# Two transformer layers on one Trainium2 core: the norm at each channel mixer's entrance taken apart, and its low parts moved behind each scaled tile

## The chip, the cores and the metric

One core of one Trainium2 chip runs the whole program. The metric is the time of one execution on the device in microseconds; the times given are medians of runs, and the profile is of one execution of its own.

## What is computed

A trunk of two layers on a sequence of 1024 tokens with 1024 features. Each layer is a token mixer (forgetting attention in layer 0, gated linear attention in layer 1) and a dense channel mixer, each behind an RMS norm that is scaled and shifted by a vector. The change lies where the channel mixer begins:

```python
def rms_norm(x, g):
    xf = x.astype(jnp.float32)
    y = xf * lax.rsqrt(jnp.mean(xf * xf, axis=-1, keepdims=True) + EPS)
    return (y * g.astype(jnp.float32)).astype(x.dtype)

def modulate(h, shift, scale):
    return h * (1.0 + scale[:, None, :]) + shift[:, None, :]

def swiglu(h, w_in, w_out):
    gate, up = jnp.split(h @ w_in, 2, axis=-1)
    return (jax.nn.silu(gate) * up) @ w_out
```

## The kernel before

Features lie on the 128 partitions, in eight blocks of 128; tokens lie along the free axis, in two halves of 512. An exact float32 product is made of three: each operand is kept as a high part that TensorE takes at full rate and a low part, the rest. `mm3` issues the three: L290 is weight high by tile high, L291 weight high by tile low, L292 weight low by tile high. One matmul is 128x128 weights by 128x512. So a tile's low part is first read by L291 and a weight's low part first by L292. Parts of activations are made by `split_t`: the high part on ScalarE (L1436, L1439), the low part on VectorE (L1437 without a shift, L1440 with one). Parts of weights come the same way, L174 on ScalarE and L175 on VectorE, from tiles that the feed loads.

The channel mixer (`ffn`, L1397) multiplies in a scheme of the Strassen kind: token halves and feature halves make four blocks, B11 and B21 of the first half of the tokens, B12 and B22 of the second, each of four tiles. Differences T1 = B12 − B11 and T2 = B22 − T1, and later T3 and T4, feed products that need fewer multiplications. The first group of hidden features is done without the scheme, in eight *plain tiles* (`plain_tile`, L1587), each of 24 matmuls into one bank of PSUM: three on the first half of the tokens, then four on the second, and one more on the first. The scheduler interleaves plain tiles where their operands come late. Their ends, L1605 and L1576, add or multiply from PSUM on VectorE.

The scaled tiles need the norm. Squares of the features are added up (`SumSq`, L741), for this norm into two roots; `sums` (L751) multiplies each root with a column of ones, four matmuls of one column each (L756), all into one tile sp. L699 on VectorE and a power on GpSimd (L700) make the four columns of inverse roots; L709 spreads them into rb, 128x512 in PSUM, with four matmuls. `normed` (L1432) is x by a column by rb, on VectorE.

For the first half of the tokens that has been done before the plain tiles begin. For the second half, `rms_rows` and `second_half` come ahead of the plain tiles in the code, and `GK=(4, 7)` holds products of the second plain tile behind the sums and rb: from its fourth step on they are issued behind the sums, from its seventh behind rb. `second_half` makes B12 and B22 (tile yb, then its parts), the differences from GpSimd (L1474) and VectorE (L1476), and the parts of T1 and T2. A scheduler puts the instructions of each engine into one fixed order, by data and by these gates. Each engine then runs its own list in that order.

PSUM has eight banks: six in the ring pj, two in psr; the plain tiles' ring pin uses them all.

Of the kernel before, what the change touches and what calls it, by code (L numbers as in the profile page):

```python
# [9 lines left out]
F32 = mybir.dt.float32  # L10
# [43 lines left out]
def trunk(ctx, tc, x, c, ada_w, ada_b, norm1_g, norm2_g, ffn_w_in, ffn_w_out,  # L54
          fox_w_in, fox_b_f, fox_w_out, gla_w_in, gla_w_a2, gla_b_a, gla_g_o,
          gla_w_out, final_g, out, dbg=None, stop=None):
    nc = tc.nc
# [51 lines left out]
    def psl(t, n=1):  # L109
        return slice(t * P, (t + n) * P)  # L110
# [51 lines left out]
    ones = cst.tile([P, 1], F32, name="ones")  # L162
# [126 lines left out]
    def mm3(ps, ah, al, bh, bl, start, stop):  # L289
        nc.tensor.matmul(ps, ah, bh, start=start, stop=False)  # L290
        nc.tensor.matmul(ps, ah, bl, start=False, stop=False)  # L291
        nc.tensor.matmul(ps, al, bh, start=False, stop=stop)  # L292
# [128 lines left out]
    def last_of(e):  # L421
        return next(i for i in reversed(nc.cur_bb.bb.instructions) if i.engine == ENG[e])
# [243 lines left out]
    def last_ins():  # L666
        return nc.cur_bb.bb.instructions[-1]
# [19 lines left out]

    sp_ins, rb_ins, root_ins = [], [], {}
    LATE1 = 7
    GK = (4, 7)  # L690
    SPM, RBM = (3, 4)

    def rms_cols(ss, nm, psr, n=4):

        ss.sums(psr)
        sp = ss.sp
        sp_ins.append(last_ins())
        rs = sm.tile([P, n], F32, tag="rs", name=f"rs{nm}")
        nc.vector.tensor_scalar(rs, sp, 1.0 / D, EPS, op0=ALU.mult, op1=ALU.add)  # L699
        nc.gpsimd.tensor_tensor(rs, rs, mhalf[:, 0:n], op=ALU.pow)  # L700
        root_ins.update(D=last_of("D"), G=last_of("G"))
        return rs

    def rms_rows(ss, nm, psr):

        rs = rms_cols(ss, nm, psr)
        rb = psr([P, HALF], F32, f"rb{nm}")
        for t in range(4):
            nc.tensor.matmul(rb[:, psl(t)], rs[:, t:t + 1].to_broadcast([P, P]), ident, start=True, stop=True)  # L709
        rb_ins.append(last_ins())  # L710
        return rb
# [29 lines left out]
    class SumSq:  # L741


        def __init__(self, v, hf, late, one=True):
            w = slice(256 * (hf % 2), 256 * (hf % 2) + 256) if hf > 1 else slice(0, HALF)
            self.v = [v[i][:, w] for i in ((1, 3, 2, 5, 7, 6, 3, 4) if hf else range(8))]
            self.late = late
            self.n = 2 if hf > 1 else 4
            self.roots = [self.v[0]] if one else [self.v[0], self.v[6]]

        def sums(self, psr):  # L751

            self.sp = psr([P, self.n], F32, "sp")
            for r in self.roots:
                for t in range(self.n):
                    nc.tensor.matmul(self.sp[:, t:t + 1], r[:, psl(t)], ones, start=r is self.roots[0] and t == 0,  # L756
                                     stop=r is self.roots[-1] and t == self.n - 1)

        def __call__(self, m, xk):
            v = self.v  # L760
# [29 lines left out]
    sr, tr, orr, pj = ps_rings(2, 3, 1, 2)  # L790
# [307 lines left out]
    for n, (d, hf) in enumerate(rest0):  # L1098
# [23 lines left out]
        if n in late_tr:  # L1122
            tp, i = late_tr[n]
# [273 lines left out]
    def ffn(l, oh, xs, slots, nm, mid, norm_end, each=None):  # L1397
# [32 lines left out]
        def normed(y, k, hf, rb):  # L1430

            nc.vector.scalar_tensor_tensor(y, xs[k][:, hsl(hf)], acol(l, 1, k), rb, op0=ALU.mult, op1=ALU.mult)  # L1432

        def split_t(t, y, shift=None):
            if shift is None:
                nc.scalar.copy(hi(t), y)  # L1436
                nc.vector.tensor_sub(lo(t), y, hi(t).bitcast(F32))  # L1437
# [15 lines left out]
        last_chunk(4, 4, oh, xs, l, 2, nm, sv, norm, one=False)  # L1453
        dump(f"xa{l}", xs)
        sg = opr_["sg"]
        rb = rms_rows(ss1[0], f"{l}11", psr)
        block("B22", H_SL[0:4])
        block("B12", H_SL[4:8])
        block("T1", H_SL[8:12])
        block("T2", H_SL[12:16])  # L1460
        B12, B22, T1, T2 = b["B12"], b["B22"], b["T1"], b["T2"]
        yv_ = Views(slots["to"], 2, [HALF], f"yb{l}").v
        y12, y22 = yv_[:4], yv_[4:]
        y11, y21 = ya[:4], ya[4:]

        def second_half():
            for k in range(4):
                normed(y12[k], k, 1, rb)
                split_t(B12[k], y12[k], sh(k))
            for k in range(4):  # L1470
                normed(y22[k], k + 4, 1, rb)
                split_t(B22[k], y22[k], sh(k + 4))
            for k in range(4):
                nc.gpsimd.tensor_sub(y11[k], y12[k], y11[k])  # L1474
                split_t(T1[k], y11[k])
                nc.vector.tensor_sub(y11[k], y22[k], y11[k])  # L1476
                split_t(T2[k], y11[k], sh(k + 4))
# [101 lines left out]
        B11, B21 = b["B11"], b["B21"]  # L1579


        pin = Ring(psp, list(pj.q) + list(psr.q))
        gs = [Group(*g) for g in GROUPS]
        second_half()
        wgs = [[[None, None], [None, None]] for _ in range(2)]

        def plain_tile(kind, m, hf, after=()):  # L1587
            wg = wgs[kind]
            ps = pin([P, HALF], F32, f"p{l}")
            for k in range(8):  # L1590
# [629 lines left out]
```

## Time and profile before

| | |
|---|---|
| runs | 2376.99, 2379.86, 2381.57 us; median 2379.86 |
| the profiled execution | 2379.58 us |
| its span | 2377.9 us |
| mean granted TensorE clock | 0.997 |
| instructions | 35,724 |

In the rows, PE is TensorE's matmuls, PEld its weight loads, DVE VectorE, ACT ScalarE, POOL GpSimd. A row of the timeline has start, duration, engine, line, operation, output and inputs, shape, and how many instructions are drawn together; in brackets stands the idle time ahead of it and what ended it. A row of the waits has the total, how often and the longest, in us. A window has each engine's busy time with the number of instructions, the granted clock (1.00 is full speed), and the DMA's share and rate. Times count from the start of the span; the stretch of the change lies near 655 us in layer 0 and near 1723 us in layer 1.

### The profile page before, as it was taken

How to read it: one execution, taken by the hardware profiler on the slowest of the kernel's cores; microseconds unless marked ns; L12 is line 12 of the kernel's file. 1: busy time of each engine (PE TensorE's matmuls, PEld its weight loads, DVE VectorE, ACT ScalarE, POOL GpSimd, SP SyncE). 2: the span in 40 equal slices, each digit the busy share in tenths (PEclk: the TensorE clock that was granted, in tenths of full speed). 3: DMA queues.
4: the chain of work that ended last, by engine and by line, in shares of the span. 5: the costliest groups of instructions: out<-in, count | busy, mean ns of one | idle time of the engine just before them, and what ended most of it. 6: DMA issues, size and time to landing. Idle time of an engine off the chain costs nothing.

```text
span 2377.9 us, 35724 instructions
## 1 busy us (share of the span) xinstructions
PE 2352.7 (99%) x12256; PEld 2004.9 (84%) x12256; DVE 1780.2 (75%) x2992; ACT 1129.3 (47%) x2178; POOL 1042.7 (44%) x976
## 2 busy tenths in 40 slices
PE   8999999999999999999999999999999999999998
PEld 7988888888888888888888889898888888888888
DVE  6577787886698878876788775655697877865787
ACT  6666566575443333345325655443444333345326
POOL 1334444533435666653363321212336666643262
PEclk9999999999999999999999999999999999999999
DMA  7423333332425544457665332334434544457664
GB/s 250 152 80 115 106 120 94 120 125 98 143 101 181 180 164 171 161 189 255 230 210 168 104 108 86 98 110 140 144 102 157 181 151 151 151 192 256 229 199 147
DMA packets 336366, 363.47 MB, mean 153 GB/s; under 512 B 24924, under 2 KB 278008, under 8 KB 336184
## 3 DMA queue, kind: packets, MB, share of 16 engines
q1 hardware_dynamic: 336184, 361.18, 45.6%
q8 instruction: 97, 1.59, 0.3%
q14 instruction: 85, 0.70, 0.1%
HBM read 268.22 MB, written 92.86 MB: 152 GB/s over the span
## 4 chain that ended last, share of the span: by engine, by line
PE 85%; DVE 8%; ACT 2%; issue 2%; DMA 2%; POOL 1%; SPq 1%; DVEq 0%; POOLq 0%; ACTq 0%
PE p_b L292 16%; PE p_b L290 16%; PE p_b L291 16%; PE o_b L1230 2%; PE t_b L1216 2%; PE qk_b L290 1%; PE qk_b L291 1%; PE qk_b L292 1%; PE vps_b L292 1%; PE vps_b L290 1%; PE vps_b L291 1%; PE gr_b L290 1%; PE s_b L1184 1%; PE gr_b L291 1%; PE gr_b L292 1%
## 5 line engine op out<-in xcount | busy, mean ns | idle before, releaser
L175 DVE TENSOR_TENSOR o_s<-xv_s,o_s 128x512 fp32r<-128x512 f32 (+1 forms) x376 | 327.3, 876 | 66.2 <-ACT o_s L174 65.7
L174 ACT CAST o_s<-xv_s 128x512 fp32r<-128x512 f32 (+1 forms) x376 | 216.6, 587 | 300.9 <-PE p_b L292 248.7
L291 PE MATMUL p_b<-B,o_s 128*128 128x512 f32 x608 | 237.2, 390 | 0.0
L292 PE MATMUL p_b<-B,o_s 128*128 128x512 f32 x608 | 236.7, 390 | 0.0
L290 PE MATMUL p_b<-B,o_s 128*128 128x512 f32 x608 | 235.9, 391 | 0.7 <-DVE x L1576 0.7
L895 POOL TENSOR_TENSOR ex_s<-xv_s,xv_s 128x512 f32<-128x512 f32 (+1 forms) x64 | 87.5, 1367 | 284.2 <-DMA xv_s<-in_ffn_w_in_dram 114.1
L1196 POOL TENSOR_SCALAR lp_s<-lp_s,st 128x128 f32<-128x128 f32 (+7 forms) x128 | 97.6, 766 | 248.9 <-DVE st L1195 230.7
L291 PE MATMUL p_b<-T,o_s 128*128 128x512 f32 x480 | 186.8, 389 | 0.0
L290 PE MATMUL p_b<-T,o_s 128*128 128x512 f32 x480 | 186.7, 389 | 0.0
L292 PE MATMUL p_b<-T,o_s 128*128 128x512 f32 x480 | 181.3, 389 | 0.0
L290 PEld LDWEIGHTS p_b<-B,o_s 128*128 128x128 f32 x608 | 114.4, 188 | 24.6 <-DVE x L1576 1.1
L291 PEld LDWEIGHTS p_b<-B,o_s 128*128 128x128 f32 x608 | 114.4, 188 | 24.1 <-DVE B L1440 0.4
L292 PEld LDWEIGHTS p_b<-B,o_s 128*128 128x128 f32 x608 | 114.4, 188 | 23.8
L1194 ACT ACTIVATE lp_s<-lp_s,st 128x128 f32<-128x128 f32 (+7 forms) x128 | 99.4, 777 | 60.9 <-DVE st L1190 59.8
L897 POOL TENSOR_TENSOR xv_s<-ex_s,xv_s 128x512 f32<-128x512 f32 (+1 forms) x64 | 86.7, 1355 | 63.9 <-DVE o_s L175 61.4
L174 ACT CAST pt_s<-t_b 128x512 fp32r<-128x512 f32 (+1 forms) x160 | 79.8, 547 | 72.7 <-PE t_b L1216 71.2
L1576 DVE TENSOR_TENSOR ex_s<-ex_s,p_b 128x512 f32<-128x512 f32 x140 | 93.8, 682 | 22.0 <-PE p_b L292 21.7
L175 DVE TENSOR_TENSOR pt_s<-t_b,pt_s 128x512 fp32r<-128x512 f32 (+1 forms) x160 | 96.3, 630 | 15.7 <-ACT pt_s L174 15.2
L231 POOL TENSOR_TENSOR w_l_s<-w__s,w_h_s 128x256 fp32r<-128x256 f32 x90 | 70.1, 807 | 85.0 <-ACT w_h_s L227 54.2
L907 POOL TENSOR_TENSOR xv_s<-xv_s,xv_s 128x512 f32<-128x512 f32 x40 | 54.1, 1352 | 120.2 <-issue 72.5
L291 PEld LDWEIGHTS p_b<-T,o_s 128*128 128x128 f32 x480 | 90.1, 188 | 18.8
L290 PEld LDWEIGHTS p_b<-T,o_s 128*128 128x128 f32 x480 | 90.1, 188 | 18.7
(1973 smaller groups left out, 7435.2 us busy)
## 6 DMA issues: line engine op xcount, KB each, us to landing
xv_s<-in_ffn_w_in_dram SPq DMA_DIRECT2D x176, 256.0 KB, 3.2
hid_B<-x SPq DMA_DIRECT2D x70, 512.0 KB, 2.6
ad_s<-in_ada_w_dram SPq DMA_DIRECT2D x384, 64.0 KB, 2.3
hid_T<-x SPq DMA_DIRECT2D x36, 512.0 KB, 2.8
xv_s<-in_ffn_w_out_dram SPq DMA_DIRECT2D x96, 192.0 KB, 5.0
ada_s<-in_ada_w_dram SPq DMA_DIRECT2D x96, 128.0 KB, 2.8
xv_s<-in_ffn_w_out_dram SPq DMA_DIRECT2D x40, 256.0 KB, 2.9
T2o<-hid_T SPq DMA_DIRECT2D x18, 512.0 KB, 9.0
```

The lines of the kernel that those rows point to most:

```text
L174: nc.scalar.copy(hi, src)
L175: nc.vector.tensor_sub(lo, src, hi.bitcast(F32))
L231: (nc.gpsimd if i < 3 else nc.vector).tensor_sub(lo[:, cs], rw[:, cs], hi[:, cs].bitcast(F32))
L290: nc.tensor.matmul(ps, ah, bh, start=start, stop=False)
L291: nc.tensor.matmul(ps, ah, bl, start=False, stop=False)
L292: nc.tensor.matmul(ps, al, bh, start=False, stop=stop)
L895: nc.gpsimd.tensor_add(s1, a21, a22)
L897: nc.gpsimd.tensor_sub(a11, s1, a11)
L907: nc.gpsimd.tensor_sub(r[A12], r[A12], r[A11])
L1194: nc.scalar.activation(lp, lp, AF.Exp, bias=mcur, scale=-1.0, accum_out=st[:, qi, 2:3])
L1196: nc.gpsimd.tensor_scalar(lp, lp, st[:, qi, 3:4], 1.0, op0=ALU.mult, op1=ALU.mult)
L1576: nc.vector.tensor_add(d, d if src is None else dest(G, src), ps)
```

## The change

`rms_rows` is cut into `rms_cols` and `rms_spread`. `sums` can stop behind the first root and go on later. `plain_tile` can issue given steps behind one of its own steps, and what follows is then issued behind them. Root 0's sums come behind step 3 of the second plain tile, root 1's with the inverse roots behind step 5, and rb behind step 1 of the third (`KS = (3, 5, 1)`). The blocks of the second half and `second_half` stand behind these three plain tiles; pin has six banks until then and the other two afterwards. `second_half` now issues each tile's low part behind the next tile's `normed`, which waits for the low part two back, and T1's parts behind the low part `LK + k`. Both layers have it. The core of the diff:

```diff
-    GK = (4, 7)
+    KS, LK = (3, 5, 1), 3
...
     def rms_rows(ss, nm, psr):
-        rs = rms_cols(ss, nm, psr)
+        return rms_spread(rms_cols(ss, nm, psr), nm, psr)
+
+    def rms_spread(rs, nm, psr):
         rb = psr([P, HALF], F32, f"rb{nm}")
         for t in range(4):
             nc.tensor.matmul(rb[:, psl(t)], rs[:, t:t + 1].to_broadcast([P, P]), ident, start=True, stop=True)
...
-        def sums(self, psr):
-            self.sp = psr([P, self.n], F32, "sp")
-            for r in self.roots:
+        def sums(self, psr, upto=None):
+            if not self.done:
+                self.sp = psr([P, self.n], F32, "sp")
+            upto = len(self.roots) if upto is None else upto
+            for i in range(self.done, upto):
                 for t in range(self.n):
...
-        rb = rms_rows(ss1[0], f"{l}11", psr)
-        def second_half():
-            for k in range(4):
-                normed(y12[k], k, 1, rb)
-                split_t(B12[k], y12[k], sh(k))
-            for k in range(4):
-                normed(y22[k], k + 4, 1, rb)
-                split_t(B22[k], y22[k], sh(k + 4))
...
-        pin = Ring(psp, list(pj.q) + list(psr.q))
+        pin = Ring(psp, list(pj.q))
...
+                if k in dict(steps):
+                    at = last_ins()
+                    with tc.issue_after(at):
+                        dict(steps)[k]()
+                    after = (last_of("P"),)
...
         plain_tile(0, 0, 0)
-        plain_tile(0, 1, 0, ((GK[0], sp_ins[-1]), (GK[1], rb_ins[-1])))
-        plain_tile(1, 0, 0, ((0, rb_ins[-1]),))
+        plain_tile(0, 1, 0, (), ((KS[0], lambda: ss1[0].sums(psr, 1)),
+                                 (KS[1], lambda: r1.append(rms_cols(ss1[0], f"{l}11", psr)))))
+        plain_tile(1, 0, 0, (), ((KS[2], spread),))
+        def second_half(rb):
+            y = y12 + y22
+            lows = []
+            for k in range(9):
+                if k < 8:
+                    with tc.issue_after(lows[k - 2]) if k > 1 else ExitStack():
+                        normed(y[k], k, 1, rb)
+                if k:
+                    split_t((B12 + B22)[k - 1], y[k - 1], sh(k - 1))
+                    lows.append(last_of("D"))
+            for k in range(4):
+                nc.gpsimd.tensor_sub(y11[k], y12[k], y11[k])
+                with tc.issue_after(lows[LK + k]):
+                    split_t(T1[k], y11[k])
+                nc.vector.tensor_sub(y11[k], y22[k], y11[k])
+                split_t(T2[k], y11[k], sh(k + 4))
+        second_half(r1[1])
+        pin.q.extend(psr.q)
```

Lines behind the diff have other numbers in the new kernel: L756 is L761 there, L709 L712, L1432 L1438, L1437 L1443, L1440 L1446, L1605 L1591, L1576 L1559.

The first place is TensorE's list in layer 0 around the second plain tile. Here sp_b is the tile of the sums, ss_s_7077 and ss_s_7078 are the two roots, p_b_1 and p_b_2 plain tiles on the first half of the tokens, B their tiles and o_s weights. Before:

```order
L756 MATMUL sp_b_3_7463<-ones,ss_s_7077 128x1 x4
L756 MATMUL sp_b_3_7463<-ones,ss_s_7078 128x1 x4
L290 MATMUL p_b_2_7658<-B_7085,o_s_4_7671 128x512
L291 MATMUL p_b_2_7658<-B_7085,o_s_4_7671 128x512
L292 MATMUL p_b_2_7658<-B_7085,o_s_4_7671 128x512
L290 MATMUL p_b_2_7658<-B_7086,o_s_4_7671 128x512
L291 MATMUL p_b_2_7658<-B_7086,o_s_4_7671 128x512
L292 MATMUL p_b_2_7658<-B_7086,o_s_4_7671 128x512
L290 MATMUL p_b_2_7658<-B_7087,o_s_4_7671 128x512
L291 MATMUL p_b_2_7658<-B_7087,o_s_4_7671 128x512
L292 MATMUL p_b_2_7658<-B_7087,o_s_4_7671 128x512
L709 MATMUL rb_b_4_7475<-ident,rs_7472 128x128 x4
```

In the changed kernel the list reads, from root 0's sums on:

```order
L292 MATMUL p_b_1_7543<-B_7088,o_s_2_7429 128x512
L761 MATMUL sp_b_3_7586<-ones,ss_s_7077 128x1 x4
L290 MATMUL p_b_2_7573<-B_7085,o_s_4_7591 128x512
L291 MATMUL p_b_2_7573<-B_7085,o_s_4_7591 128x512
L292 MATMUL p_b_2_7573<-B_7085,o_s_4_7591 128x512
L290 MATMUL p_b_2_7573<-B_7086,o_s_4_7591 128x512
L291 MATMUL p_b_2_7573<-B_7086,o_s_4_7591 128x512
L292 MATMUL p_b_2_7573<-B_7086,o_s_4_7591 128x512
L761 MATMUL sp_b_3_7586<-ones,ss_s_7078 128x1 x4
L290 MATMUL p_b_2_7573<-B_7087,o_s_4_7591 128x512
L291 MATMUL p_b_2_7573<-B_7087,o_s_4_7591 128x512
```

Six matmuls of 512 columns now stand between the two roots' sums, and six more between the second sums and rb (L712). Root 0's sums stand six rows further back in TensorE's list than before, root 1's twelve and rb nine; the first product on the second half of the tokens stands in the same row as before.

The second place is VectorE's list in layer 0 from L699 on. Tiles yb are the scaled tiles, B their low parts, T those of T1. Before:

```order
L699 TENSOR_SCALAR rs_7472<-sp_b_3_7463 128x4
L1432 TENSOR_SCALAR yb_s_7496<-x_0_6282,amul,rb_b_4_7475 128x512
L1432 TENSOR_SCALAR yb_s_7496<-x_1_6283,amul,rb_b_4_7475 128x512
L1432 TENSOR_SCALAR yb_s_7497<-x_2_6284,amul,rb_b_4_7475 128x512
L1432 TENSOR_SCALAR yb_s_7497<-x_3_6285,amul,rb_b_4_7475 128x512
L1432 TENSOR_SCALAR yb_s_7498<-x_4_6286,amul,rb_b_4_7475 128x512
L1432 TENSOR_SCALAR yb_s_7498<-x_5_6287,amul,rb_b_4_7475 128x512
L1432 TENSOR_SCALAR yb_s_7499<-x_6_6288,amul,rb_b_4_7475 128x512
L1432 TENSOR_SCALAR yb_s_7499<-x_7_6289,amul,rb_b_4_7475 128x512
L1440 TENSOR_SCALAR B_7484<-yb_s_7496,modc,B_7484 128x512
L1440 TENSOR_SCALAR B_7485<-yb_s_7496,modc,B_7485 128x512
L1440 TENSOR_SCALAR B_7486<-yb_s_7497,modc,B_7486 128x512
```

and in the changed kernel:

```order
L699 TENSOR_SCALAR rs_7606<-sp_b_3_7586 128x4
L1438 TENSOR_SCALAR yb_s_7672<-x_0_6282,amul,rb_b_4_7627 128x512
L1438 TENSOR_SCALAR yb_s_7672<-x_1_6283,amul,rb_b_4_7627 128x512
L1446 TENSOR_SCALAR B_7660<-yb_s_7672,modc,B_7660 128x512
L1438 TENSOR_SCALAR yb_s_7673<-x_2_6284,amul,rb_b_4_7627 128x512
L1446 TENSOR_SCALAR B_7661<-yb_s_7672,modc,B_7661 128x512
L1438 TENSOR_SCALAR yb_s_7673<-x_3_6285,amul,rb_b_4_7627 128x512
L1446 TENSOR_SCALAR B_7662<-yb_s_7673,modc,B_7662 128x512
L1591 TENSOR_TENSOR sg_s_7571<-sg_s_7571,p_b_3_7617 128x512
L1438 TENSOR_SCALAR yb_s_7674<-x_4_6286,amul,rb_b_4_7627 128x512
L1446 TENSOR_SCALAR B_7663<-yb_s_7673,modc,B_7663 128x512
L1438 TENSOR_SCALAR yb_s_7674<-x_5_6287,amul,rb_b_4_7627 128x512
```

Low parts that stood behind all eight scaled tiles now stand between them.

The third place is VectorE's list some sixty operations later, ahead of the low parts of the weight tiles o_s_14 and o_s_16, which TensorE reads next. Before:

```order
L490 TENSOR_SCALAR ad_s_7894<-ad_s_7894,c_164 128x256
L1605 TENSOR_TENSOR sg_s_7688<-sg_s_7688,p_b_8_7836 128x512
L175 TENSOR_TENSOR o_s_14_7956<-xv_s_7387,o_s_14_7956 128x512
L175 TENSOR_TENSOR o_s_15_7975<-xv_s_7387,o_s_15_7975 128x512
L1437 TENSOR_TENSOR x_3_6285<-sg_s_7688,x_3_6285 128x512
L1437 TENSOR_TENSOR x_4_6286<-sg_s_7688,x_4_6286 128x512
L175 TENSOR_TENSOR o_s_16_7998<-xv_s_7385,o_s_16_7998 128x512
L1576 TENSOR_TENSOR x_0_6282<-x_0_6282,p_b_3_7978 128x512
```

and in the changed kernel:

```order
L175 TENSOR_TENSOR o_s_19_8070<-xv_s_7386,o_s_19_8070 128x512
L1559 TENSOR_TENSOR x_1_6283<-x_0_6282,p_b_5_8033 128x512
L175 TENSOR_TENSOR o_s_15_7975<-xv_s_7387,o_s_15_7975 128x512
L490 TENSOR_SCALAR ad_s_7894<-ad_s_7894,c_164 128x256
L1591 TENSOR_TENSOR sg_s_7615<-sg_s_7615,p_b_7_7802 128x512
L1591 TENSOR_TENSOR sg_s_7615<-sg_s_7615,p_b_8_7836 128x512
L175 TENSOR_TENSOR o011s_s_17_8028<-ex_s_7382,o011s_s_17_8028 128x512
L175 TENSOR_TENSOR o_s_14_7956<-xv_s_7387,o_s_14_7956 128x512
L1443 TENSOR_TENSOR x_3_6285<-sg_s_7615,x_3_6285 128x512
L1443 TENSOR_TENSOR x_4_6286<-sg_s_7615,x_4_6286 128x512
L1559 TENSOR_TENSOR x_0_6282<-x_0_6282,p_b_2_7959 128x512
L175 TENSOR_TENSOR o_s_16_7998<-xv_s_7385,o_s_16_7998 128x512
```

Of what stands here ahead of o_s_16, the low parts of o_s_19 and o011s_s and the additions of p_b_3, p_b_5 and p_b_2 (L1559) stood behind it before; o_s_14's low part has moved behind o_s_15's and these, but p_b_2's. Layer 1's lists have the same pattern. TensorE's list takes the products of these weights, from the first with o_s_14 on, in the same rows as before, but for one matmul.

More of the change, by code (lines that the diff above doesn't have):

```diff
@@ L747, in __init__ @@
             self.late = late
-            self.n = 2 if hf > 1 else 4
+            self.n, self.done = (2 if hf > 1 else 4), 0
             self.roots = [self.v[0]] if one else [self.v[0], self.v[6]]
-        def sums(self, psr):
-            self.sp = psr([P, self.n], F32, "sp")
-            for r in self.roots:
+        def sums(self, psr, upto=None):
[3 more added lines that the diff above has]
+            for i in range(self.done, upto):
                 for t in range(self.n):
-                    nc.tensor.matmul(self.sp[:, t:t + 1], r[:, psl(t)], ones, start=r is self.roots[0] and t == 0,
-                                     stop=r is self.roots[-1] and t == self.n - 1)
+                    nc.tensor.matmul(self.sp[:, t:t + 1], self.roots[i][:, psl(t)], ones, start=i == 0 and t == 0,
+                                     stop=i == len(self.roots) - 1 and t == self.n - 1)
+            self.done = upto
         def __call__(self, m, xk):
@@ L1579, in ffn, with plain_tile @@
         B11, B21 = b["B11"], b["B21"]
-        pin = Ring(psp, list(pj.q) + list(psr.q))
+        pin = Ring(psp, list(pj.q))
         gs = [Group(*g) for g in GROUPS]
-        second_half()
         wgs = [[[None, None], [None, None]] for _ in range(2)]
-        def plain_tile(kind, m, hf, after=()):
+        def plain_tile(kind, m, hf, after=(), steps=()):
             wg = wgs[kind]
```

31 lines of the change are left out of this document (14 added, 17 removed).

## The prediction

> **What bounds the kernel now.** The profile's first table, read first:
>
> ```profile
> PE 2352.7 (99%) x12256; PEld 2004.9 (84%) x12256; DVE 1780.2 (75%) x2992; ACT 1129.3 (47%) x2178; POOL 1042.7 (44%) x976
> ```
>
> PE is the bound: 25 us of the span are not PE's, and the change touches two short stretches, one per layer. So the question is what PE waits for there. The waits of PE, asked for layer 0 from 600 to 760 us, and then for layer 1 from 1690 to 1820:
>
> ```profile
> PE p_b L290 <- DVE x L1576: 0.7, 1, 0.7
> PE sp_b L756 <- DVE ss_s L773: 0.2, 1, 0.2
> ```
>
> ```profile
> PE sp_b L756 <- DVE ss_s L773: 0.3, 1, 0.3
> ```
>
> The named waits are 0.9 us in layer 0 and 0.3 us in layer 1. PE's timeline in layer 0 (start, us busy) shows what the norm costs besides:
>
> ```profile
> 655.17 0.95 PE L756 MATMUL sp_b<-ones,ss_s 128*128 128x1 f32 x8
> 656.36 1.05 PE L756 MATMUL sp_b<-ones,ss_s 128*128 128x1 f32 x8 [0.24 <-DVE ss_s L773]
> 657.27 0.48 PE L290 MATMUL p_b<-B,o_s 128*128 128x512 f32 x1
> 657.59 0.40 PE L291 MATMUL p_b<-B,o_s 128*128 128x512 f32 x1
> 657.83 0.39 PE L292 MATMUL p_b<-B,o_s 128*128 128x512 f32 x1
> 658.05 0.40 PE L290 MATMUL p_b<-B,o_s 128*128 128x512 f32 x1
> 659.42 1.05 PE L709 MATMUL rb_b<-ident,rs 128*128 128x128 f32 x8
> ```
>
> The two roots' sums, back to back, take 657.27 − 655.17 = 2.10 us from the products; a 512-column product then takes 0.23 us. Layer 1 has the same rows, but the granted clock (the last column but two of the windows) falls to half behind the sums:
>
> ```profile
> 1722.74 0.95 PE L756 MATMUL sp_b<-ones,ss_s 128*128 128x1 f32 x8
> 1724.89 0.47 PE L290 MATMUL p_b<-B,o_s 128*128 128x512 f32 x1
> ```
>
> ```profile
> core 0: us, PE busy (x) PEld busy (x) DVE busy (x) ACT busy (x) POOL busy (x), PEclk, DMA share, GB/s
> 1725.00:1726.00 1.00, 1.00 (x5) 0.82 (x5) 0.16 (x1) 0.00 (x0) 0.69 (x1) 0.74 0.00 0
> 1726.00:1727.00 1.00, 1.00 (x4) 0.80 (x3) 0.00 (x0) 0.00 (x0) 0.32 (x1) 0.50 0.00 0
> 1727.00:1728.00 1.00, 1.00 (x4) 0.72 (x3) 0.00 (x0) 0.00 (x0) 0.00 (x0) 0.50 0.00 0
> 1728.00:1729.00 1.00, 1.00 (x6) 0.90 (x5) 0.00 (x0) 0.00 (x0) 0.00 (x0) 0.55 0.00 0
> ```
>
> From the four means, (0.26 + 0.50 + 0.50 + 0.45) us of work are lost: **1.7 us**, the largest single cost that the old place of the norm has. Layer 0's like stretch kept clock 1.00.
>
> Then DVE, which makes the scaled second half. Its share of the span is 75%, but two windows of layer 0, read under the same header, have it busy for all of their ten microseconds:
>
> ```profile
> 670.00:680.00 10.00, 10.00 (x46) 8.29 (x45) 10.00 (x17) 3.79 (x6) 0.00 (x0) 1.00 0.03 12
> 700.00:710.00 10.00, 10.00 (x46) 8.29 (x45) 10.00 (x13) 3.53 (x6) 5.29 (x5) 1.00 0.53 182
> ```
>
> Here the 75% says nothing: whatever starts later on DVE ends later, until its queue runs dry.
>
> **Step 1: sums apart.** In the new order six 512-column products stand between the roots' sums, and six between these and rb. Root 1's addition then has time to end, so the waits of 0.24 and 0.3 go. PE saves between 0 and 0.5 us a layer (2.10 less two undisturbed runs of 0.8); I take 0.3. No long stretch of short matmuls is left, so layer 1's clock spell of 1.7 us goes; bounds 0 and 1.7, and I take 1.7.
>
> **Step 2: DVE starts later.** Rows of the way from the sums to the first normed tile, DVE and then POOL, layer 0, and layer 1's first normed:
>
> ```profile
> 657.45 0.16 DVE L699 TENSOR_SCALAR rs<-sp_b 128x4 f32<-128x4 f32 x1 [1.14 <-PE sp_b L756]
> 660.52 5.36 DVE L1432 SCALAR_TENSOR_TENSOR yb_s<-x,amul,rb_b 128x512 f32<-128x512 f32 x8 [2.90 <-PE rb_b L709]
> 1729.71 0.75 DVE L1432 SCALAR_TENSOR_TENSOR yb_s<-x,amul,rb_b 128x512 f32<-128x512 f32 x1 [4.49 <-PE rb_b L709]
> ```
>
> ```profile
> 657.69 1.02 POOL L700 TENSOR_TENSOR rs<-rs,mhalf 128x4 f32<-128x4 f32 x1 [1.93 <-DVE rs L699]
> ```
>
> New times of layer 0: first run at 655.17 + 6 × 0.23 = 656.5, its end at 657.3, six products to 658.8, second run to 659.65, L699 and the power to 661.1 (1.44 us as before), rb from 661.2, first normed 1.1 us behind its start (660.52 − 659.42): 662.35. That is **1.85 us later** than 660.52. Nothing hides it, as DVE is full. In layer 1 the same way takes 7.2 us from the first run's old start, 1722.74: 1729.95, only 0.25 us later, since the half clock had held rb up already.
>
> **Step 3: low parts beside POOL.** Eight normed tiles in a row read rb in PSUM and went at 0.67 us each while POOL made its four differences. The new order puts low parts (L1440, both tensors in SBUF) there. What POOL does to an operation with two SBUF tensors, the same L1437 with POOL at work and without:
>
> ```profile
> 692.03 1.77 DVE L1437 TENSOR_TENSOR T<-ya_s,T 128x512 fp32r<-128x512 f32 x1
> 695.71 0.68 DVE L1437 TENSOR_TENSOR T<-ya_s,T 128x512 fp32r<-128x512 f32 x1
> ```
>
> ```profile
> 661.41 5.08 POOL L1474 TENSOR_TENSOR ya_s<-yb_s,ya_s 128x512 f32<-128x512 f32 x4 [2.70 <-DVE yb_s L1432]
> 691.58 1.68 POOL L907 TENSOR_TENSOR xv_s<-xv_s,xv_s 128x512 f32<-128x512 f32 x1 [1.88 <-DMA xv_s<-in_ffn_w_in_dram]
> ```
>
> DVE waits until POOL's operation is through: 1.1 us. The four differences (1.27 us each) now meet the first low parts. Three low parts put off by about 0.5 us each make 1.5, where the old order lost 0.5 in its first low part; so **+1.0 us** a layer, bounds 0 and +4.4 (four meetings at 1.1).
>
> **Step 4: more in front of what PE needs.** DVE's new queue has, ahead of the low part of weight tile o_s_16, five operations of layer 0 more (low parts of o_s_19 and o011s_s, and L1576 on the products p_b_3, p_b_5 and p_b_2): 5 × 0.60 = 3.0 us by the rows' pitch. In layer 1 the same five, L488 and L490: 3.8 us. Now DVE and PE at this weight, in both layers (PE's L292 is the first that reads the low part; of layer 0 also o_s_14's pair):
>
> ```profile
> 703.75 1.28 DVE L175 TENSOR_TENSOR o_s<-xv_s,o_s 128x512 fp32r<-128x512 f32 x2
> 706.16 1.77 DVE L175 TENSOR_TENSOR o_s<-xv_s,o_s 128x512 fp32r<-128x512 f32 x1
> 1773.60 1.77 DVE L175 TENSOR_TENSOR o_s<-xv_s,o_s 128x512 fp32r<-128x512 f32 x1
> ```
>
> ```profile
> 707.80 0.39 PE L292 MATMUL p_b<-T,o_s 128*128 128x512 f32 x1
> 710.52 0.39 PE L292 MATMUL p_b<-B,o_s 128*128 128x512 f32 x1
> 717.49 0.50 PE L290 MATMUL p_b<-B,o_s 128*128 128x512 f32 x1 [0.68 <-DVE x L1576]
> 1779.69 0.39 PE L292 MATMUL p_b<-B,o_s 128*128 128x512 f32 x1
> ```
>
> Layer 0: o_s_14's low part, done at 704.4, has five more ahead too: 704.4 + 1.85 + 1.0 + 3.0 = 710.25, while PE wanted it at 707.80: a stall of 2.45 us (2.75 with PE 0.3 us early). o_s_16's: 707.9 + 5.85 = 713.75 against 710.52, **+3.2 us**, the first stall included. The late PE no longer meets the 0.68 us wait at 717.49, so layer 0 nets **+2.5**. Layer 1: 1775.3 + 0.25 + 1.0 + 3.8 = 1780.35 against 1779.69: **+0.65**, with its stalls, 2.6 us in sum, eating the 1.7 and the 0.3 that PE had won.
>
> **Step 5: the clock.** A short idle can halve the clock here, as this row and window of layer 0's attention show:
>
> ```profile
> 417.17 0.55 PE L1216 MATMUL t_b<-ident,lp_s 128*128 128x128 f32 x3 [2.03 <-POOL lp_s L1196]
> 419.00:420.00 1.00, 1.00 (x6) 0.91 (x5) 0.99 (x2) 1.00 (x2) 0.00 (x0) 0.50 0.75 183
> ```
>
> After 2.03 us of idle the spell is as long as layer 1's, so its price is 1.7 us of PE, of which the smaller wait at o_s_16 absorbs about 0.5: +1.2. Two stalls over 2 us stand in the sum. As layer 0's sums show, not each such stretch falls so; I take one spell. Bounds: none, or both (+2.4). [...]
>
> Sum, on the profiled execution: 2379.6 (span 2377.9; 0.3 us below the median 2379.9) + 2.5 + 0.65 + 1.2 = **2383.9 us**. Moving the blocks' allocation and the ring of banks behind the plain tiles issues nothing: instruction counts on each engine are those of before, and the first second-half product stands in the same row of PE's queue. I cost it at 0; bounds 0 and the 0.7 us that a late bank costs at 717.49.
>
> **The rivals.**
> - *Stalls without a clock spell*: steps 1 to 4 alone, 2382.7. For it speaks layer 0's stretch of sums at clock 1.00; against it the row at 417.17.
> - *More meetings with POOL and the clock lost in both layers*: one more meeting of 1.1 us a layer before o_s_16 and 1.2 us of clock more: 2383.9 + 2.2 + 1.2 = 2387.3, slower by 0.3%. It decides once POOL's later work falls behind DVE's two-tensor operations in the new queue; the 5.29 us of POOL in the window 700 to 710 speak for it, that the count of operations stays the same against it.
> - *DVE catches up in time, so faster*: if the low parts don't meet POOL and the feed's low parts come before PE wants them, no stall takes the place of those removed: layer 0 saves 0.3 and 0.68, layer 1 0.3 and 1.7: 2379.6 − 3.0 = 2376.6. It needs DVE to make good 5.85 us against a slack of 707.8 − 704.4 = 3.4; the full windows speak against it.
> - *Next to nothing*: half of step 4's lateness, which the gains of step 1 then balance: 2380.
>
> **How the numbers follow.** About 0.2%, 4.8 us, is what a measurement of this kernel can tell from no change: from 2375.1 to 2384.6 counts as the same. Chances: forecast 0.34, stalls alone 0.18, POOL and clock 0.26, caught up 0.12, nothing 0.10. The range 2376.5 to 2388.5 leaves out the last 1 in 10 at each end: four meetings with POOL above, the whole of step 1 at its best below. Slower by over 0.2%: all of the third case and a third of the forecast's spread, 0.26 + 0.12 = 0.38, and some 0.02 of the second: 0.40. Faster by over 0.2%: beyond even the best sum, 0.03. Within 0.2%: 0.57.
>
> **What would show it.** Right: PE's waits on L773 gone; layer 1 at clock 1.00 behind the sums; the first normed of layer 0 near 662.3; its L1440 rows of the first low parts at 1 us or more beside POOL; a new wait of PE's L292 on DVE's L175 of 2 to 3 us near 707 and one near 711, and in layer 1 near 1776; a half clock behind one of them. Wrong: no wait on L175 (then 2376 to 2378), or a wait earlier, at the first second-half products near 667, which would mean that the scaled tiles themselves come late.

## The result and the profile after

The changed kernel takes **2384.67 us** (median of 12 runs, 2381.91 to 2387.51) against 2379.25 (12 runs, 2376.99 to 2381.57): ratio **1.0024**, 95% interval 1.0017 to 1.0032, so 5.4 us slower. The forecast was 2383.9, in a range from 2376.5 to 2388.5.

TensorE's row of the profile's first table, and its waits, asked for layer 0 from 600 to 760 us and for layer 1 from 1690 to 1820:

```profile
PE 2350.3 (99%) x12256; PEld 2001.1 (84%) x12256; DVE 1777.6 (75%) x2992; ACT 1131.0 (48%) x2178; POOL 1045.4 (44%) x976
```

```profile
PE p_b L292 <- DVE o_s L175: 1.6, 1, 1.6
```

```profile
PE p_b L292 <- DVE o_s L175: 3.3, 1, 3.3
```

The waits on the roots' additions and on the bank are gone. One wait for a weight's low part stands in each layer in their place. They are at o_s_14 and at its counterpart in layer 1, in PE's timeline:

```profile
707.90 0.50 PE L292 MATMUL p_b<-T,o_s 128*128 128x512 f32 x1 [1.62 <-DVE o_s L175]
1777.49 0.50 PE L292 MATMUL p_b<-T,o_s 128*128 128x512 f32 x1 [3.28 <-DVE o_s L175]
```

The granted clock in layer 1 (last column but two), around the sums and behind the wait:

```profile
core 0: us, PE busy (x) PEld busy (x) DVE busy (x) ACT busy (x) POOL busy (x), PEclk, DMA share, GB/s
1725.00:1726.00 1.00, 1.00 (x10) 0.96 (x9) 0.00 (x0) 0.00 (x0) 0.00 (x0) 1.00 0.00 0
1726.00:1727.00 1.00, 1.00 (x6) 0.85 (x6) 0.16 (x1) 0.00 (x0) 0.57 (x1) 1.00 0.00 0
1778.00:1779.00 1.00, 1.00 (x3) 0.73 (x3) 1.00 (x3) 0.00 (x0) 0.81 (x1) 0.50 0.25 52
1779.00:1780.00 1.00, 1.00 (x4) 0.78 (x3) 1.00 (x2) 0.00 (x0) 0.47 (x1) 0.50 0.95 309
1780.00:1781.00 1.00, 1.00 (x4) 0.81 (x3) 1.00 (x3) 0.00 (x0) 0.57 (x1) 0.50 1.05 415
1781.00:1782.00 1.00, 1.00 (x5) 0.77 (x5) 0.88 (x2) 0.42 (x1) 1.00 (x1) 0.84 0.95 337
```

The half clock has left the sums and come back behind the wait.

Where the time went is read best by matching the 12,256 matmuls of both traces one by one: by how much does product n start later than in before? A stretch costs what this number grows by across it. Across layer 0's stretch (from 650 to 730 us of before) it grows by **0.87 us**, across layer 1's (1717 to 1797) by **3.45 us**, of which 1.6 is the half clock. Layer 1's trace of before had 1.7 us of half clock of its own, which the change took back. These 4.3 us are most of the 5.4; between the layers and at the start single executions differ by 1 to 2 us either way, so that the profiled execution as a whole ends only 2.3 us later.

Why is o_s_14's low part late? VectorE, ScalarE and GpSimd ahead of the first wait in layer 0 (VectorE's rows from 700.30 to 702.76 and one of ScalarE at 699.13 are left out):

```profile
693.73 0.68 DVE L175 TENSOR_TENSOR o_s<-xv_s,o_s 128x512 fp32r<-128x512 f32 x1
694.33 0.68 DVE L1443 TENSOR_TENSOR T<-ya_s,T 128x512 fp32r<-128x512 f32 x1
694.93 0.68 DVE L175 TENSOR_TENSOR o001s_s<-ex_s,o001s_s 128x512 fp32r<-128x512 f32 x1
695.53 0.68 DVE L175 TENSOR_TENSOR o_s<-xv_s,o_s 128x512 fp32r<-128x512 f32 x1
696.14 1.28 DVE L1443 TENSOR_TENSOR T<-ya_s,T 128x512 fp32r<-128x512 f32 x2
697.34 0.68 DVE L1559 TENSOR_TENSOR x<-x,p_b 128x512 f32<-128x512 f32 x1
699.26 1.12 DVE L1443 TENSOR_TENSOR x<-sg_s,x 128x512 fp32r<-128x512 f32 x1 [1.24 <-ACT x L1442]
704.92 1.24 DVE L175 TENSOR_TENSOR o011s_s<-ex_s,o011s_s 128x512 fp32r<-128x512 f32 x1 [0.89 <-ACT o011s_s L174]
706.09 1.76 DVE L175 TENSOR_TENSOR o_s<-xv_s,o_s 128x512 fp32r<-128x512 f32 x1
```

```profile
698.61 0.62 ACT L1442 CAST x<-sg_s 128x512 fp32r<-128x512 f32 x1 [5.75 <-POOL sg_s L1518]
704.27 0.62 ACT L174 CAST o011s_s<-ex_s 128x512 fp32r<-128x512 f32 x1 [3.79 <-POOL ex_s L901]
704.80 0.62 ACT L174 CAST o_s<-xv_s 128x512 fp32r<-128x512 f32 x1
```

```profile
693.88 4.69 POOL L1518 TENSOR_TENSOR sg_s<-sg_s 128x512 f32<-128x512 f32 x1 [11.95 <-DVE sg_s L1591]
698.54 1.29 POOL L913 TENSOR_TENSOR xv_s<-xv_s,xv_s 128x512 f32<-128x512 f32 x1
702.94 1.29 POOL L901 TENSOR_TENSOR ex_s<-xv_s,xv_s 128x512 f32<-128x512 f32 x1 [3.12 <-DMA xv_s<-in_ffn_w_in_dram]
```

Read it from the end. o_s_14's low part (706.09) stands behind o011s_s's, which waited for ScalarE's high part (704.27), which waited 3.79 us for a sum on GpSimd (L901, 702.94), which waited 3.12 us for the weights. Their load was issued only at 699.85, when L913 (698.54 to 699.83) was through. All the while o_s_14's own high part (704.80) stood in ScalarE's list behind o011s_s's. And L913 was late, since it stood behind L1518: that is an operation of 1.3 us (1.29 at the shortest of its ten in this trace, 1.62 in their median) that took 4.69, beside an unbroken run of VectorE's two-tensor operations; it ended 1.23 us after VectorE took up one that reads PSUM (697.34). **VectorE was not full here**: it idled 2.1 us (1.24 and 0.89 in the rows).

### The profile page after: what moved, and what is told of

Read it like the earlier page. It is cut to its first block, busy times and chain, and to the rows that moved or that the text cites. A ratio compares the mean times of both kernels' runs of the same rounds, so it can differ in the third digit from the quotient of the medians.

```text
span 2380.2 us, 35732 instructions
## 1 busy us (share of the span) xinstructions
PE 2350.3 (99%) x12256; PEld 2001.1 (84%) x12256; DVE 1777.6 (75%) x2992; ACT 1131.0 (48%) x2178; POOL 1045.4 (44%) x976
## 4 chain that ended last, share of the span: by engine, by line
PE 83%; DVE 7%; issue 2%; ACT 2%; DMA 2%; POOL 1%; SPq 1%; DVEq 0%; POOLq 0%; ACTq 0%
PE p_b L292 15%; PE p_b L290 15%; PE p_b L291 15%; PE o_b L1236 2%; PE t_b L1222 2%; PE qk_b L290 2%; PE qk_b L291 2%; PE qk_b L292 2%; PE vps_b L292 1%; PE vps_b L290 1%; PE vps_b L291 1%; PE gr_b L290 1%; PE gr_b L291 1%; PE s_b L1190 1%; PE s_b L1191 1%
## 5 line engine op out<-in xcount | busy, mean ns | idle before, releaser
L175 DVE TENSOR_TENSOR o_s<-xv_s,o_s 128x512 fp32r<-128x512 f32 (+1 forms) x376 | 328.8, 879 | 65.4 <-ACT o_s L174 64.7
L901 POOL TENSOR_TENSOR ex_s<-xv_s,xv_s 128x512 f32<-128x512 f32 (+1 forms) x64 | 84.8, 1324 | 284.2 <-DMA xv_s<-in_ffn_w_in_dram 114.1
L292 PEld LDWEIGHTS p_b<-T,o_s 128*128 128x128 f32 x480 | 90.5, 189 | 24.5 <-DVE o_s L175 5.8
L1559 DVE TENSOR_TENSOR ex_s<-ex_s,p_b 128x512 f32<-128x512 f32 x140 | 93.7, 681 | 21.3 <-PE p_b L292 21.2
L175 DVE TENSOR_TENSOR pt_s<-t_b,pt_s 128x512 fp32r<-128x512 f32 (+1 forms) x160 | 96.3, 630 | 15.7 <-ACT pt_s L174 15.2
L290 PEld LDWEIGHTS p_b<-T,o_s 128*128 128x128 f32 x480 | 90.4, 188 | 19.0 <-ACT o_s L174 0.3
L291 PEld LDWEIGHTS p_b<-T,o_s 128*128 128x128 f32 x480 | 90.4, 188 | 18.8
```

Source lines behind the costliest of these rows:

```text
L175: nc.vector.tensor_sub(lo, src, hi.bitcast(F32))
L901: nc.gpsimd.tensor_add(s1, a21, a22)
L1559: nc.vector.tensor_add(d, d if src is None else dest(G, src), ps)
```

## The experiments

Two theories at first. *A*: the place in the lists costs, since o_s_14's parts stand behind o011s_s's, which wait for GpSimd. *B*, the prediction's: VectorE has too much work ahead. Each ratio is to the kernel before in runs on the same chip. The kernel before took 2378.8 to 2379.3 us on these chips, so medians of different experiments compare to about half a microsecond, besides the intervals.

**1. o_s_14 ahead of o011s_s.**

```diff
+        if gr == (0, 1) and ab == (1, 1):
+            front_.update(A=last_of("A"), D=last_of("D"))
...
+            if gr == (1, 1):
+                es.enter_context(tc.issue_after(front_["A"]))
+                es.enter_context(tc.issue_after(front_["D"]))
             split(t[:, 0], t[:, 1], s1)
```

> The changed kernel, but the parts of weight o011s_s are issued behind those of o_s_14 on ScalarE and VectorE. Theory A (place in the list: o_s_14's parts stand behind o011s_s's, which wait for a sum that GpSimd makes late): the waits on L175 of 1.6 us in layer 0 and 3.3 us in layer 1 go but for at most 0.5 each, and with the second the half clock behind it (1.6 us); 5 to 6.5 us less than the changed kernel, so 2378 to 2380. Theory B (VectorE has too much work ahead, as the prediction had it): only one operation of 0.6 us is taken out of the way, so about 1 us less in each layer, 2382 to 2384.

Measured: 2385.81 us (six runs), 1.0026 (1.0014 to 1.0037): no gain, and outside what either theory gave. The waits moved on:

```profile
712.69 0.50 PE L292 MATMUL p_b<-B,o_s 128*128 128x512 f32 x1 [2.33 <-DVE o_s L175]
1778.54 0.50 PE L292 MATMUL p_b<-T,o_s 128*128 128x512 f32 x1 [0.57 <-DVE o_s L175]
1784.43 0.50 PE L292 MATMUL p_b<-B,o_s 128*128 128x512 f32 x1 [2.85 <-DVE o_s L175]
```

They now stand 12 products later, at o_s_16, which is still behind o011s_s. Theory A as put (one pair in the wrong order) falls, and B's gain of 1 us a layer did not come. No half clock stands behind the two waits of over 2 us here: the products behind them go on at 0.23 us each.

**2. The sums alone**: the changed kernel with the old body of `second_half`.

```diff
-            for k in range(9):
-                if k < 8:
-                    with tc.issue_after(lows[k - 2]) if k > 1 else ExitStack():
-                        normed(y[k], k, 1, rb)
-                if k:
-                    split_t((B12 + B22)[k - 1], y[k - 1], sh(k - 1))
+            for k in range(4):
+                normed(y12[k], k, 1, rb)
+                split_t(B12[k], y12[k], sh(k))
...
```

> The changed kernel with the old body of second_half: sums in two runs and rb between plain tiles, but all eight scaled tiles first and their low parts behind them. VectorE's list has o_s_14 ahead of o011s_s again. Theory A: no wait on L175; the waits on L773 and the half clock behind layer 1's sums stay away; 2 to 3 us less than before, 2376 to 2377.5. Theory B: VectorE begins 1.85 us late in layer 0, with 3.4 us of slack at o_s_14, so no stall there either, but the 0.7 us wait at a late bank stays; 2377 to 2378. A rival that the late start of VectorE is itself the loss: a wait on L175 of 1 us or more in layer 0 and 2380 or above.

Measured: 2382.33, 1.0013 (1.0004 to 1.0022). Theories A and B both missed it. The rival came with its time (2380 or above), but not at L175: the wait is at the first low part of all (VectorE, then PE, layer 0):

```profile
662.88 5.36 DVE L1438 SCALAR_TENSOR_TENSOR yb_s<-x,amul,rb_b 128x512 f32<-128x512 f32 x8 [2.35 <-PE rb_b L712]
668.15 2.54 DVE L1446 SCALAR_TENSOR_TENSOR B<-yb_s,modc,B 128x512 fp32r<-128x512 f32 x3
```

```profile
669.41 0.50 PE L291 MATMUL p_b<-B,o_s 128*128 128x512 f32 x1 [1.76 <-DVE B L1446]
```

VectorE's late start is paid at once, 1.8 us a layer. The other half of the change is what removes this wait. There is none on L175 here, so the lists of weights' parts turn with the new body, not with the sums.

**3. The low parts alone**: the kernel before with the new body (edit 2 the other way).

> The kernel before with the new body of second_half alone: old sums and gates, but each low part behind the next scaled tile. The lists have o_s_14 behind o011s_s, as in the changed kernel. Theory A: waits on L175 of 1.5 to 3 us in both layers, less in layer 1, since TensorE comes 2 us later to it, with the half clock of layer 1's sums kept; 2382 to 2385, so about 3 to 6 us more than before. Theory B: VectorE begins 1.85 us sooner than in the changed kernel in layer 0, stalls of under 1 us; 2380 to 2381.

Measured: 2385.82, 1.0028 (1.0018 to 1.0038), 0.8 us above A's range and far above B's: waits on L175 of 2.3 and 2.8 us, each with a half clock behind it. The new body carries the whole loss without the new sums.

**4. The kernel before with o_s_14 put behind o011s_s.**

```diff
+        if gr == (1, 1):
+            for e, i in back_:
+                tc.add_manual_dep(i, last_of(e).name, mybir.DependencyInfo(
+                    mybir.DependencyClass.NoSync, mybir.DependencyReason.DATA), reason="order")
```

> The kernel before, with o_s_14's parts issued behind o011s_s's on ScalarE and VectorE and nothing else changed by hand. Theory A: the place alone makes a wait on L175 of 2 to 3 us in each layer, since o011s_s's low part ended at 709.7 us against the 707.8 at which TensorE wants o_s_14's; 2383 to 2386. If the place costs nothing without the new second half: 2379 to 2380.

Measured: 2382.6, 1.0016 (1.0008 to 1.0025), just under A's range. In layer 0 TensorE waits 0.6 us for o011s_s's high part and 1.4 for o_s_14's low part, in layer 1 0.8 us at a bank and not on L175. The place by itself costs, 1.6 and 1.4 us by the matched products, but in layer 0 less than expected and in layer 1 in another way.

**5. o_s_16 ahead of o011s_s too** (edit 1 with o_s_16 in the place of o_s_14).

> The changed kernel, with the parts of weight o011s_s issued behind those of o_s_16, so behind o_s_14's too. With o_s_14 alone ahead the stall came 12 products later, at o_s_16, which still stood behind o011s_s. Theory A2 (what waits for GpSimd's late sum holds all that stands behind it on ScalarE and VectorE): no wait on L175 over 0.5 us in either layer and no half clock there; 4 to 6 us less than the changed kernel, 2378 to 2381. Theory B (VectorE's work itself is late): the wait at o_s_16 stays at 2 us or more, 2383 to 2386. A stall that only moves on to o011s_s's own products: a wait of 1 to 2 us there, 2381 to 2383.

Measured: 2382.89, 1.0018 (1.0009 to 1.0027), 1.8 us under the changed kernel by the medians, though the two intervals overlap; A2's 2378 to 2381 and its waits of at most 0.5 us did not come. PE's waits in layer 0, and in layer 1:

```profile
PE p_b L292 <- DVE o_s L175: 1.1, 1, 1.1
```

```profile
PE p_b L290 <- DVE x L1567: 1.7, 1, 1.7
PE p_b L292 <- DVE o_s L175: 1.0, 2, 0.6
```

No half clock. So the place is a part; another part, waits of 1.1 us in layer 0 and 2.7 in layer 1, stays. VectorE's rows ahead of o_s_16's low part, which ended at 711.11, show what it is:

```profile
705.94 3.47 DVE L1451 TENSOR_TENSOR x<-sg_s,x 128x512 fp32r<-128x512 f32 x2
```

L1451 is L1443 of the changed kernel. Two such operations unhindered take 1.3 us (1.28 at 697.16 in the same trace); these took 2.2 more, beside GpSimd, which was at work from 704.18 on with hardly a gap. With the low part ahead of them (1.05 us for 0.68) and o_s_16's own (1.17 for 0.68) VectorE lost 3.1 us, and without that would have been through at 708.1, before TensorE asked at 710.0. In layer 1 six operations ahead of the addition that frees the bank took 9.55 us for 3.74, so 5.8 us more, with GpSimd busy for at least 92% of each microsecond from 1773 to 1783. So by subtraction these waits too are meetings with GpSimd; no run shows it.

**6. One of GpSimd's operations on VectorE.**

```diff
-                nc.gpsimd.tensor_sub(v["B11"], v["B12"], v["B11"])
+                (nc.vector if i == 0 else nc.gpsimd).tensor_sub(v["B11"], v["B12"], v["B11"])
```

> The changed kernel with one subtraction a layer (the first group's hidden difference B12 - B11, 4.7 us on GpSimd beside a run of VectorE's operations) on VectorE instead; o_s_14 and o_s_16 stay behind o011s_s in the lists. Theory A2 with GpSimd shut out by VectorE's run as the cause: GpSimd's sum for o011s_s starts 2 to 3 us sooner, the waits on L175 shrink from 1.6 and 3.3 us to under 1 us each; 2380 to 2382. Theory B: 0.6 us more of VectorE's work, so the waits grow by 0.6 us each; 2385 to 2386. If only the landing of the weights sets the sum's start: waits as in the changed kernel, 2384 to 2385.

Measured: 2381.81, 1.0013 (1.0004 to 1.0022), 2.9 us under the changed kernel by the medians and within the range of A2, though not quite by its way. GpSimd in layer 0:

```profile
698.43 2.83 POOL L913 TENSOR_TENSOR xv_s<-xv_s,xv_s 128x512 f32<-128x512 f32 x1 [14.41 <-issue]
704.22 1.29 POOL L901 TENSOR_TENSOR ex_s<-xv_s,xv_s 128x512 f32<-128x512 f32 x1 [2.96 <-DMA xv_s<-in_ffn_w_in_dram]
```

Beside VectorE's run it is now the next operation that takes long (2.83 us for 1.29), and the sum starts only 0.8 us sooner by the matched products (702.94 in a trace that stood 2.1 us earlier). The wait in layer 0 falls from 1.6 to 0.9 us; layer 1's becomes two, 1.2 and 1.6 us, with no half clock behind them.

**7. Only two low parts between the scaled tiles**, the other six behind the eighth.

> The changed kernel with only the first two low parts behind the next scaled tile, the other six behind the eighth, as before. With none there (sums_only) TensorE waited 1.8 us a layer for the first low part; with all there the lists of the weights' parts turned. Here the lists have o_s_14 and o_s_16 ahead of o011s_s. If these two are the costs: no wait on L1446 or L175 over 0.5 us; the gains of the sums in two runs are left, 1 us in layer 0 and 2 us in layer 1; 2376 to 2378. If VectorE's late start is paid in any case: a wait of 1 us or more at the third low part or at a weight, 2380 to 2383.

Measured: 2380.66, 1.0009 (1.0 to 1.0018). No wait on L175; 0.2 us a layer on L1446, and 1.3 and 0.3 us at banks that VectorE empties (L1559). Better than the changed kernel by 4 us, but not 2376 to 2378. The second case came by its time. The late start is still paid at the first low parts, 0.9 us a layer by the matched products; in two_lows_sooner (10), where VectorE starts 0.7 us sooner, that is 0.3 us. The waits at banks stay there, at 1.4 and 0.3 us, so they come from something else.

**8. Sums only, sooner**: experiment 2 with `KS = (3, 4, 0)`.

> sums_only with KS = (3, 4, 0): three matmuls instead of six between the sums of the two roots, and rb three matmuls sooner, 0.7 us. The wait for the first low part falls from 1.8 us to 1.1 us a layer, with 1.4 us saved over both layers against sums_only: 2380.5 to 2381.5. If TensorE then waits for root 1's sum or for the powers instead: a wait of 0.2 to 0.5 us on L779 or L700 and 2381 to 2382.5. If the half clock of layer 1 comes back, because the sums stand closer: 1.7 us more.

Measured: 2379.87, 1.0005 (0.9996 to 1.0014): a wait on L1446 of 1.1 us a layer in place of 1.8, as expected. By the medians it is 2.5 us less than sums_only where 1.4 were expected, a difference that the intervals do not resolve; the matched products give 1.25.

**9 to 11. Variants of it**: the first low part between scaled tiles; the first two; and both roots' sums together, `KS = (3, 3, 0)`.

> Sums and rb as in sums_sooner (KS = (3, 4, 0)), and the first low part alone behind the second scaled tile, the other seven behind the eighth. sums_sooner waited 1.1 us a layer for that first low part, two_lows 0.2 for a later one and up to 1.3 at banks that VectorE empties. If the late first low part was the last cost: no wait on L1446 over 0.3 us, and 2376.5 to 2378, 1 to 2.5 us under the kernel before. If the turned lists of the weights' parts cost as in two_lows (waits on L1559 of 1 us in layer 0): 2378.5 to 2380.

> The same with the first two low parts between scaled tiles. If VectorE's late start made two_lows wait, 0.7 us less of it brings the waits on L1446 and L1559 from 1.5 and 0.5 us to 0.5 and 0 us, and 2377 to 2379. If these waits come from the order of the parts: as two_lows, 2380 to 2381.

> sums_sooner with both roots' sums back to back in the first place (KS = (3, 3, 0)), rb where it was. If keeping the short sums apart is what keeps the clock: a half clock behind the sums in one of the two layers in the profiled run, and 0.5 to 2 us more than sums_sooner, 2380 to 2382, with the wait on L779 back at 0.2 us. If the clock has nothing to do with it: within 0.5 us of sums_sooner, 2379.5 to 2380.5.

Measured: 2379.41, 1.0000 (0.9992 to 1.0009); 2380.56, 1.0007 (0.9998 to 1.0016); 2380.01, 1.0002 (0.9993 to 1.0011). The first has no wait on L1446 or L175, only one of 1.1 us at a bank in layer 0, and still only equals the kernel before; that is the second case of its expectation. So it is with two_lows_sooner, whose waits at banks stay. Putting the sums together again brought no half clock in either layer, the second case again.

**12. The changed kernel with `KS = (3, 4, 0)`.**

> The changed kernel with KS = (3, 4, 0) and nothing else: VectorE starts 0.7 us sooner, all low parts behind their tiles, o_s_14 and o_s_16 still behind o011s_s in the lists. If the lists and GpSimd's late sum are the cost: the waits on L175 stay over 1 us in each layer, 2383 to 2385. If VectorE's late start is the cost there too: the waits shrink by 0.7 us each, or go, 2380 to 2382.5.

Measured: 2384.18, 1.0023 (1.0015 to 1.0032). PE's waits, layers 0 and 1:

```profile
PE p_b L292 <- DVE o_s L175: 1.8, 1, 1.8
```

```profile
PE p_b L292 <- DVE o_s L175: 2.8, 1, 2.8
```

Starting VectorE 0.7 us sooner does not shorten them. Nor does the start in lows_only, 1.85 us sooner than in the changed kernel by the prediction's working (waits of 2.3 and 2.8 us). With all low parts between the tiles, the late start is not what makes them.

What each kernel's two stretches cost against before's trace, by the matched products, in us (layer 1 of that trace holds 1.7 us of half clock behind the sums, and so does o14_behind's, so what the others show there is 1.7 us less than their own cost):

| kernel | layer 0 | layer 1 |
|---|---|---|
| changed | +0.87 | +3.45 |
| o14_first | +1.33 | +2.13 |
| sums_only | +0.77 | +0.19 |
| sums_sooner | +0.34 | −0.63 |
| lows_only | +2.97 | +3.01 |
| o14_behind | +1.62 | +1.39 |
| o16_first | +0.24 | +1.67 |
| t1_on_vector | +0.13 | +1.49 |
| all_lows_sooner | +2.38 | +2.66 |
| one_low_sooner | +0.43 | −1.39 |
| two_lows | +1.56 | −0.17 |
| two_lows_sooner | +0.79 | −0.98 |
| sums_together | +0.33 | −0.63 |

## Why the prediction held, and where its steps failed

The likeliest case came, with its kind of stall, its place in the program and one half clock, and its sum, 4.35 us over the profiled execution, is close to the two stretches' 4.3. That closeness is luck, since the parts were off both ways: layer 0 was forecast at +2.5 and came at +0.87, layer 1 without its clock spell at +0.65 and came at +1.85 (3.45 less 1.6), and the spell at 1.2 came at 1.6. In mechanism the loss is nearer to the second rival, more meetings with GpSimd, than to a longer queue.

*Step 1, sums apart*: right. The waits on L773 are gone, layer 1's sums keep clock 1.00, and PE gains 0.3 us in layer 0 and, besides the clock, 0.2 in layer 1 by the matched products (0.3 taken):

```profile
655.14 0.94 PE L761 MATMUL sp_b<-ones,ss_s 128*128 128x1 f32 x8
657.43 0.95 PE L761 MATMUL sp_b<-ones,ss_s 128*128 128x1 f32 x8
```

The 1.7 us of clock was, however, counted as if each execution had it. The clock fell to half behind back-to-back sums in 2 of the 8 stretches traced (before, lows_only, o14_behind, sums_together; two layers each), behind sums apart in none of 20. On these few it is worth about 0.4 us a layer (2 of 8 times 1.7), and even 2 of 8 against 0 of 20 could be chance. The median of before can hold less of it than its trace; no run shows how much.

*Step 2, VectorE starts later*: right in size. The first scaled tile of layer 0 starts at 660.92 in a trace that runs 1.40 us ahead there, 662.32 against the 662.35 worked out (layer 1: 1728.70 and 1.18, so 1729.88 against 1729.95); sums_only shows the same delay as a wait of its own.

*Step 3, low parts beside POOL*: right. Four rows of VectorE in layer 0:

```profile
660.92 1.41 DVE L1438 SCALAR_TENSOR_TENSOR yb_s<-x,amul,rb_b 128x512 f32<-128x512 f32 x2 [2.35 <-PE rb_b L712]
662.47 1.20 DVE L1446 SCALAR_TENSOR_TENSOR B<-yb_s,modc,B 128x512 fp32r<-128x512 f32 x1
664.25 1.12 DVE L1446 SCALAR_TENSOR_TENSOR B<-yb_s,modc,B 128x512 fp32r<-128x512 f32 x1
665.95 1.12 DVE L1446 SCALAR_TENSOR_TENSOR B<-yb_s,modc,B 128x512 fp32r<-128x512 f32 x1
```

The first three low parts, beside GpSimd's four differences (661.82 to 668.24), take 1.1 to 1.2 us instead of the 0.74 of the fourth (668.25), 1.2 us in sum where 1.5 was taken.

*Step 4, more in front of what PE needs*: this step failed in its mechanism. It counted five operations at 0.6 us in a queue that is always full, and got a stall of 2.75 us in layer 0 and 2.6 in layer 1. Measured were 1.62 and 3.28. The queue was not full, and had not been full in before: of the window from 700 to 710, busy throughout, at least 2.8 us were meetings with GpSimd (L490 took 1.51 us for 0.47 at 701.72, L175 1.77 and 1.40 for 0.68 at 706.16 and 708.45, with operations of GpSimd from 701.27, 705.80 and 708.01 on beside them). A busy engine in these views can be one that is held. In the changed kernel o_s_14's low part of layer 0 ended at 707.85 in a trace that ran 1.40 us ahead, so at 709.25. Less the 2.1 us of idle and the 0.6 and 1.1 us that the last two operations took over 0.68 beside GpSimd (1.24 and 1.76), VectorE's work alone would have been through at about 705.5, before TensorE asked (707.8 in before), where the step had 710.25. Between 682 and 694 us GpSimd had nothing to run (11.95 us idle), and from 694 on it was itself shut out (4.69 us), so it cost VectorE less than in before, where between 688 and 701 four operations took 1.38 to 1.78 us beside it, for 0.34 to 0.74 unhindered; VectorE then waited for a weight sum that GpSimd made late. So what stands in front costs its own waits and meetings besides its 0.6 us. In layer 1 VectorE waited only 0.1 us for the weight's sum (and 1.24 us for L1518's result before); there it was the meetings, which came right ahead of o_s_14's low part. VectorE's rows, then GpSimd's:

```profile
1772.94 1.56 DVE L175 TENSOR_TENSOR o111s_s<-ex_s,o111s_s 128x512 fp32r<-128x512 f32 x1
1774.43 1.35 DVE L488 TENSOR_SCALAR ad_s<-ad_s,c 128x256 f32<-128x256 f32 x1
1775.70 1.74 DVE L175 TENSOR_TENSOR o_s<-xv_s,o_s 128x512 fp32r<-128x512 f32 x1
```

```profile
1772.21 1.74 POOL L1519 TENSOR_TENSOR sg_s<-sg_s,sg_s 128x512 f32<-128x512 f32 x1
1773.91 1.71 POOL L902 TENSOR_TENSOR xv_s<-xv_s 128x512 f32<-128x512 f32 x1
1775.59 1.31 POOL L1524 TENSOR_TENSOR sg_s<-sg_s,sg_s 128x512 f32<-128x512 f32 x1
```

Against 0.7, 0.3 and 0.7 us unhindered (0.68 for L175 at 695.53 and 0.34 for L488 at 700.30 in layer 0), these three of VectorE lost 2.9 us; with TensorE 1.9 us sooner at the place, that makes layer 1's wait the longer one. The predicted second wait at o_s_16 did not come in the changed kernel, where the first had put TensorE off; in o14_first it did.

*Step 5, the clock*: one spell was taken at 1.2 us net, one came, at 1.6. That it was one, and in which layer, the traces do not let one foretell: five of twelve such waits had one (below).

How the parts of the loss divide is settled only so far. The new body of `second_half` carries it (lows_only), the late start under it does not (all_lows_sooner), the place behind o011s_s is a part (o16_first, 1.8 us less, with overlapping intervals but shorter waits in the trace) and GpSimd's lateness is a part (t1_on_vector, 2.9 us less). That what is left in o16_first is meetings with GpSimd and not work follows only by subtraction: no kernel took GpSimd's operations out of that stretch.

## What to carry to other kernels

Before pricing an operation that a change puts ahead of a critical one in an in-order list, look for what that operation waits for: behind a wait its duration can be the smallest part of its price. Count a full engine by what its operations take unhindered, not by its busy share. When a producer is started later, look first at its very first consumer, and when work is interleaved to save that consumer, compare the order of everything behind it, since a scheduler may turn pairs far away. A gain that one trace shows as a half clock is to be counted by how often it happens, not in full.

## What the runs showed of the hardware

- **A run of VectorE's two-tensor operations held GpSimd up by as much as 3.4 us.** L1518 took 4.69 us for 1.29 while six of VectorE's operations with two SBUF inputs followed on each other without a gap (693.73 to 697.42); it ended 1.23 us behind the start of the next one, L1559 at 697.34, which reads PSUM. In layer 1 it took 4.69 us too (from 1761.66) and ended 1.23 us behind L1559 at 1765.12. In layer 0 of o14_first and o16_first the same operation took 4.68 and 4.69 us, in t1_on_vector L913 took 2.83 for 1.29, and each ended 1.23 us behind the start of that addition. That VectorE's run is what held them up is a reading of these five cases.
- **A half clock followed a wait of 1.78 us, and none a wait of 2.85 us.** Of twelve waits of 1.6 us or more in the stretches, five were followed by 3.4 us at half clock, the shortest of 1.78 us (all_lows_sooner, layer 0), while 2.85 us in o14_first was not. The wait of 1.78 us, and the clock behind it (the windows from 709 on, two left out):

```profile
709.68 0.52 PE L292 MATMUL p_b<-T,o_s 128*128 128x512 f32 x1 [1.78 <-DVE o_s L175]
```

```profile
core 0: us, PE busy (x) PEld busy (x) DVE busy (x) ACT busy (x) POOL busy (x), PEclk, DMA share, GB/s
709.00:710.00 1.00, 0.32 (x1) 0.30 (x2) 1.00 (x3) 0.11 (x1) 0.80 (x1) 1.00 0.63 242
710.00:711.00 1.00, 1.00 (x4) 0.78 (x3) 1.00 (x1) 0.20 (x1) 0.77 (x1) 0.52 1.05 397
...
713.00:714.00 1.00, 1.00 (x5) 0.81 (x4) 1.00 (x3) 0.00 (x0) 0.63 (x1) 0.77 1.05 250
```
